# Gated linear attention levels as 64 by 64 products on the two array halves, in one run per head

## The chip, the cores and the metric

The kernel runs on one core of a Trainium2 chip. The metric is the time of one execution on the device, in microseconds (us); a time given for a kernel is the median of several executions. Engines are named as in the profile: PE is the matmul engine and PEld its weight loads, DVE the vector engine, ACT the scalar engine, POOL the general engine, SP the engine that issues most DMAs. Matmuls write to PSUM, eight banks of 128 partitions by 512 float32; DVE and ACT read them there.

## The reference, cut to what matters

One decoder layer on 2048 tokens behind 16 meta tokens, width 1024. A combined projection feeds two branches, a state-space scan (SSD, 16 heads of 64 columns in 4 groups) and gated linear attention (GLA, 4 heads, keys of 128, values of 256). Gates merge the branches, and an output projection and a norm follow. The change is in the GLA branch. Within a chunk it computes

```
gc = cumsum(log_a)                                  # per channel
rel = exp(where(causal, gi[t] - gi[s], -inf))       # per t, s and channel
att = einsum('bhtk,bhsk,bhtsk->bhts', qi, ki, rel)  # scores inside the chunk
o_t = att @ v + (q * exp(g)) @ state
```

The decay between t and s differs by channel, so that `att` isn't one plain product.

## The kernel before, in words

The tokens go in four blocks of 512. For each block (the loop at L1067), a list of "pieces" projects the normed input to what one SSD group or GLA head needs (`proj_conv`, `proj_qk`, `proj_v`, `gla_gates` and so on; their matmuls are L223, L224 and L225 in `accum`, three for each float32 product whose operands are split into high and low parts). Between pieces, `step` (L1012) advances every generator that is running by one `yield`: `ssd_scan` for the four groups, `gla_scan` for the four heads. A scan has more yields than a unit has pieces, so that the last steps of one head fall between the same pieces as the first steps of the next head. After the four blocks come the gates, branch and output products (L1141 to L1349), which the change doesn't touch.

The orders of PE and of SP are written out by hand: they are that of the program (`manual_schedule`, L1066). DVE, ACT and POOL are ordered by a scheduler, which mixes instructions of the scans that are under way. Each engine runs its own order strictly; semaphores make an instruction wait for those of other engines.

A chunk of `gla_scan` has 128 tokens; a block has four chunks, taken as two pairs. The scores are found by levels, at distances 64, 32, 16, 8, 4 and 2. At each level a chunk falls into pairs of neighbouring stretches; the keys of one and the queries of the other are scaled by the decay from the border between them, so that their product gives the scores across this border. `level_in(half)` does the scaling: L858 (DVE) subtracts the border's value, L861 and L862 (ACT) take exponentials, L863 and the two L865 (DVE) multiply by keys and queries into the tile `kq`. For each pair of chunks `kq` is laid out so that one 128 by 128 product serves both: the scores of one chunk stand above the diagonal, and those of the other, transposed, below it. `level_out(half)` makes the two products of a level (L873), a float32 matmul of 128 by 128 by 128 each, into a bank of the pool `pc`. Level 64 is copied to the tile `xa` by ACT (L877); each lower level is merged into `xa` under its mask by a predicated copy on DVE (L880). Levels 64 to 4 come out in the second, third and fourth step of the scan, level 2 in the fifth.

In the fifth step, two products with a matrix of ones (L945) give the scores at distance 1 and 0. L947 merges distance 1 into `xa`; L950 spreads `xa` to the four chunks' `att` under triangular masks; L953 sets the diagonal. L956 splits `att` into high and low parts. In the sixth step, one piece later, PE transposes the two odd chunks of `att` (L960) and goes on to the state update (L965) and the outputs (L981, L982).

Buffers come from pools that rotate: `sq` (six of 128 by 512) holds the temporaries and `kq` of the levels, `att`, and the SSD scan's `dm` and `scm`; `c1` (eight of 128 by 256) holds `xa`, the states and others; `xd` (four) holds the SSD scan's `xdt`. The pool `pc` has two PSUM banks, `pt` three and `pj` three. The SSD scan's product L717 already uses 64 columns at a time: it alternates between the upper and the lower 64 rows of its output.

Of the kernel before, what the change touches and what calls it, by code (L numbers as in the profile page):

```python
# [8 lines left out]
F32 = mybir.dt.float32  # L9
# [17 lines left out]
NSQ = 6  # L27
NT4 = 5
NACT = 8
NC1 = 8  # L30
# [13 lines left out]
def trunk_kernel(ctx: ExitStack, tc: tile.TileContext, xm, xmt, w_feat, w_tok, w_v3, w_zm, w_br, w_o,  # L44
# [7 lines left out]
    def mk(pool, shape, dt, tag, **kw):  # L52
        cnt[0] += 1
        return pool.tile(shape, dt, tag=tag, name=f"{tag}_{cnt[0]}", **kw)
# [575 lines left out]
    def ssd_scan(o, g):  # L630
# [35 lines left out]
        held, intra = {}, {}  # L666

        def before(c):
# [9 lines left out]
            xdt = mk(wk, [P, 4, 64], F32, "xd", bufs=NCH)  # L678
# [7 lines left out]
            dm = mk(wk, [P, 4, P], F32, "sq", bufs=NSQ)  # L686
# [124 lines left out]
    def gla_scan(o, h, last=False):  # L811
# [30 lines left out]
        xa = mk(wk, [P, 2, P], F32, "c1", bufs=NC1)  # L842
        kqs = {}

        def level_in(half):
# [10 lines left out]
            kq = mk(wk, [P, BLK], F32, "sq", bufs=NSQ)  # L856
# [12 lines left out]
        def level_out(half):  # L869
            kq = kqs.pop(half)  # L870
            ps = bank(pc, "pc")
            for r in range(2):
                nc.tensor.matmul(ps[:, r * P:(r + 1) * P], kq[:, 2 * r * P:(2 * r + 1) * P],  # L873
                                 kq[:, (2 * r + 1) * P:(2 * r + 2) * P], start=True, stop=True)
            pv2 = ps[:, :256].rearrange("p (r t) -> p r t", t=P)
            if half == 64:
                nc.scalar.activation(xa, pv2, AF.Copy)  # L877
            else:
                mi = msk[:, LEVELS.index(half)].unsqueeze(1).to_broadcast([P, 2, P])
                nc.vector.copy_predicated(xa, mi, pv2)  # L880
# [20 lines left out]
        level_out(64)  # L901
# [6 lines left out]
        level_out(32)  # L908
        level_in(8)
        level_out(16)  # L910
        level_in(4)
        yield
        level_out(8)
        level_in(2)
        level_out(4)
# [24 lines left out]
        level_out(2)  # L940
        sums_ = []
        for hl, n in parts:
            ps = bank(pt, "pt")
            for i in range(2):
                nc.tensor.matmul(ps[:, :n], ones_r, hl[i], start=i == 0, stop=i == 1)  # L945
            sums_.append(ps)
        nc.vector.copy_predicated(xa, msk[:, len(LEVELS)].unsqueeze(1).to_broadcast([P, 2, P]),  # L947
                                  sums_[0][:, :256].rearrange("p (r t) -> p r t", t=P))
        att = mk(wk, [P, NCH, P], F32, "sq", bufs=NSQ)
        nc.vector.tensor_tensor(att.rearrange("p (r o) t -> p r o t", o=2),  # L950
                                xa.unsqueeze(2).to_broadcast([P, 2, 2, P]),
                                tris.unsqueeze(1).to_broadcast([P, 2, 2, P]), op=ALU.mult)
# [553 lines left out]
def _layout(inputs):  # L1506
# [41 lines left out]
    for i, h in enumerate(LEVELS + (1,)):  # L1548
        if i:
            cmsk[:, i] = (row // (2 * h) == col // (2 * h)) & (row // h != col // h)  # L1550
# [40 lines left out]
```

## Time and profile before

| What | us |
|---|---|
| median of 3 runs (lowest, highest) | 2210.77 (2210.52, 2213.93) |
| the profiled execution, its own time | 2209.51 |
| its span, first to last instruction | 2207.7 |
| PE busy | 2174.5 |
| DVE busy | 1553.8 |
| ACT busy | 1188.5 |
| POOL busy | 693.8 |
| PE busy in the level products L873 (384 records) | 53.4 |
| PE busy in the SSD products L717 (1024 records) | 33.4 |

A float32 matmul that isn't a transpose stands in the profile as two records, since PE passes over it twice. Matmuls are pipelined: a record lasts longer than the step from its start to the next one's start, so that what a matmul costs is read from starts. The span holds 1.8 us less than the execution's own time. The GLA steps of the four blocks lie at about 262 to 436, 610 to 779, 953 to 1122 and 1300 to 1432 us.

### The profile page before, as it was taken

The numbers are of one execution on the slowest core, as the hardware profiler recorded it, in microseconds if no ns is written. First come the engines' busy times: TensorE is split into PE (matmuls) and PEld (weight loads), VectorE is DVE, ScalarE is ACT, GpSimd is POOL, SyncE is SP. The second block draws the span as 40 slices with busy tenths as digits, with TensorE's granted clock in tenths as the row PEclk, the third lists the DMA queues.
The fourth block names the chain that finished last, engine by engine and source line by source line (L and its number), as shares of the span: only waits on it lengthen the run. The fifth ranks groups of instructions, "written<-read, shape, count | busy, mean of one in ns | idle before, by whom it ended". The sixth has DMA issues, their size and how long they took to land.

```text
span 2207.7 us, 35845 instructions
## 1 busy us (share of the span) xinstructions
PE 2174.5 (98%) x12301; PEld 1867.9 (85%) x12301; DVE 1553.8 (70%) x2871; ACT 1188.5 (54%) x2767; POOL 693.8 (31%) x689
## 2 busy tenths in 40 slices
PE   7999999999999999999999999999999999999998
PEld 7999889888888988888988888878888888888887
DVE  5786675677577676658677666674789955789876
ACT  5666655466455456545465554464644545554544
POOL 5444433222222122221222100166233374324341
PEclk9999999999999999999999999999999999999999
DMA  9766775667778677778677664376768866787753
GB/s 316 254 228 235 255 271 211 218 217 244 257 253 265 210 227 230 249 257 274 208 223 238 215 216 161 124 265 214 246 221 297 304 223 216 240 286 255 255 187 121
DMA packets 313702, 518.00 MB, mean 235 GB/s; under 512 B 28080, under 2 KB 162480, under 8 KB 313520
## 3 DMA queue, kind: packets, MB, share of 16 engines
q1 hardware_dynamic: 247008, 419.89, 58.3%
q10 hardware_dynamic: 65872, 93.74, 11.6%
q8 instruction: 96, 1.57, 0.3%
q0 software_dynamic: 640, 2.10, 0.2%
q14 instruction: 86, 0.70, 0.1%
HBM read 368.42 MB, written 147.19 MB: 234 GB/s over the span
## 4 chain that ended last, share of the span: by engine, by line
PE 86%; DVE 4%; ACT 3%; DMA 3%; POOL 1%; issue 1%; SPq 1%; POOLq 0%; ACTq 0%; DVEq 0%
PE pj L223 19%; PE pj L225 19%; PE pj L224 19%; PE pt L225 4%; PE pt L224 4%; PE pt L223 4%; PE pc L223 2%; PE pc L224 2%; PE pc L225 2%; PE pc L873 2%; PE pc L717 1%; PE pc L701 1%; PE pc L981 1%; PE pc L700 1%; DVE acc L612 1%
## 5 line engine op out<-in xcount | busy, mean ns | idle before, releaser
L223 PE MATMUL pj<-ue,whl 128*128 128x512 f32 (+2 forms) x672 | 236.7, 352 | 2.3 <-ACT acc L608 2.2
L224 PE MATMUL pj<-ue,whl 128*128 128x512 f32 (+2 forms) x672 | 228.9, 341 | 0.0
L225 PE MATMUL pj<-ue,whl 128*128 128x512 f32 (+2 forms) x672 | 228.5, 340 | 0.0
L223 PE MATMUL pj<-uo,whl 128*128 128x512 f32 x512 | 206.0, 402 | 0.0
L225 PE MATMUL pj<-uo,whl 128*128 128x512 f32 x512 | 199.9, 390 | 0.0
L224 PE MATMUL pj<-uo,whl 128*128 128x512 f32 x512 | 199.5, 390 | 0.0
L223 PE MATMUL pj<-b,a 128*128 128x512 f32 (+1 forms) x484 | 187.4, 387 | 0.5 <-DVE io L1304 0.5
L224 PE MATMUL pj<-b,a 128*128 128x512 f32 (+1 forms) x484 | 187.4, 387 | 0.0
L225 PE MATMUL pj<-b,a 128*128 128x512 f32 (+1 forms) x484 | 187.4, 387 | 0.0
L612 DVE SCALAR_TENSOR_TENSOR acc<-cin,hcw,acc 128x512 f32<-128x512 f32 (+1 forms) x192 | 156.1, 813 | 29.2 <-ACT acc L608 27.5
L1157 POOL TENSOR_TENSOR as<-ar,ar 128x512 f32<-128x512 f32 x38 | 58.3, 1534 | 371.4 <-DMA ar<-in_w_br 124.7
L83 POOL TENSOR_TENSOR wr<-wr 128x256 f32<-128x256 f32 x80 | 69.7, 871 | 332.2 <-DMA wr<-y 142.0
L1186 DVE TENSOR_TENSOR a<-ar,a 128x512 fp32r<-128x512 f32 x160 | 132.1, 834 | 58.8 <-ACT a L1185 57.8
L223 PEld LDWEIGHTS pj<-ue,whl 128*128 128x128 f32 x672 | 127.2, 189 | 18.3 <-ACT acc L608 3.1
L186 POOL TENSOR_TENSOR whl<-wr,whl 128x512 fp32r<-128x512 f32 (+1 forms) x76 | 102.6, 1357 | 122.0 <-ACT whl L184 93.4
L225 PEld LDWEIGHTS pj<-ue,whl 128*128 128x128 f32 x672 | 127.1, 189 | 14.4
L224 PEld LDWEIGHTS pj<-ue,whl 128*128 128x128 f32 x672 | 127.7, 190 | 13.3
L1186 DVE TENSOR_TENSOR a<-as,a 128x512 fp32r<-128x512 f32 x120 | 104.8, 875 | 41.5 <-ACT a L1185 38.2
L1185 ACT ACTIVATE a<-ar 128x512 fp32r<-128x512 f32 x160 | 99.1, 626 | 58.6 <-PE pt L225 22.1
L1220 ACT ACTIVATE sn<-pj 128x512 f32<-128x512 f32 x118 | 70.2, 595 | 110.8 <-PE pj L225 71.0
L224 PE MATMUL pt<-b,a 128*128 128x512 f32 x320 | 124.5, 389 | 0.0
L225 PE MATMUL pt<-b,a 128*128 128x512 f32 x320 | 124.5, 389 | 0.0
(335 smaller groups left out, 6367.9 us busy)
## 6 DMA issues: line engine op xcount, KB each, us to landing
whl<-k_s SPq DMA_DIRECT2D x96, 512.0 KB, 4.1
whl<-k_g SPq DMA_DIRECT2D x96, 512.0 KB, 4.5
whl<-k_v SPq DMA_DIRECT2D x36, 512.0 KB, 3.8
wr<-in_w_feat SPq DMA_DIRECT2D x64, 256.0 KB, 4.1
k_s<-whl SPq DMA_DIRECT2D x32, 512.0 KB, 3.8
cb<-cumd SPq DMA_DIRECT2D x64, 256.0 KB, 4.7
y<-gg ACTq DMA_DIRECT2D x64, 256.0 KB, 4.2
k_g<-whl SPq DMA_DIRECT2D x32, 512.0 KB, 3.7
```

The source lines that it names most:

```text
L83: nc.gpsimd.tensor_tensor(o, x, y, op=ALU.subtract)
L186: nc.gpsimd.tensor_tensor(hl[:, 1], raw, hl[:, 0].bitcast(F32), op=ALU.subtract)
L223: nc.tensor.matmul(ps, sh, mh, start=first, stop=False, **kw)
L224: nc.tensor.matmul(ps, sh, ml, start=False, stop=False, **kw)
L225: nc.tensor.matmul(ps, sl, mh, start=False, stop=last, **kw)
L612: convd[:] = [nc.vector.scalar_tensor_tensor(acc, cin[:, k:k + tt], hcw[:, ti, k:k + 1], acc, op0=ALU.mult, op1=ALU.add)]
L700: nc.tensor.matmul(ps[:, :256], cf[:, a:a + P], s_ssd[:, g], start=True, stop=True)
L873: nc.tensor.matmul(ps[:, r * P:(r + 1) * P], kq[:, 2 * r * P:(2 * r + 1) * P], kq[:, (2 * r + 1) * P:(2 * r + 2) * P], start=True, stop=True)
L1157: nc.gpsimd.tensor_tensor(s1, a21, a22, op=ALU.add)
L1185: nc.scalar.activation(t[:, 0], src, AF.Copy)
L1186: latest[:] = [nc.vector.tensor_tensor(t[:, 1], src, t[:, 0].bitcast(F32), op=ALU.subtract)]
L1220: nc.scalar.activation(sn, self.ps[n, "a"], AF.Copy)
```

## The change

**The products.** `level_out` goes. `levels_out(att)` makes the products of all six levels in one run, in the fifth step, where level 2 alone was before. Each 128 by 128 product becomes two of 64 columns by 64 columns, since two of its quadrants hold everything that the level's mask lets through: those beside the diagonal for level 64, those on it for the others. The stationary operand is 64 columns wide; the first of the two writes the output's partitions 0 to 63, the second 64 to 127, on the two halves of the array. A head has 24 such products in place of 12. They go to two `pc` banks at once, the first for levels 64 to 8, the second for 4 and 2.

**The merge.** A level now has 64 columns a pair of chunks. Level 64 goes straight to its places in `att` by two ACT copies of 64 partitions, and the opposite places are zeroed by two POOL memsets. ACT copies level 32 to `xa` (64 columns, a pool of its own with one buffer), and DVE merges the other four levels (L892). Distance 1 is merged, and `xa` spread to `att`, in two instructions of 64 partitions each (L957 and L960).

**The buffers.** A pool `kq` with six buffers now holds the `kq` tiles, `dm`, and `xdt` (two chunks to a buffer); `sq` goes from six buffers to three, `c1` from eight to six, and `xd` goes.

```diff
-NSQ = 6
+NSQ = 3
+NKQ = 6
-NC1 = 8
+NC1 = 6
...
-            xdt = mk(wk, [P, 4, 64], F32, "xd", bufs=NCH)
+            if c % 2 == 0:
+                pair[:] = [mk(wk, [P, 2, 4, 64], F32, "kq", bufs=NKQ)]
+            xdt = pair[0][:, c % 2]
...
-            dm = mk(wk, [P, 4, P], F32, "sq", bufs=NSQ)
+            dm = mk(wk, [P, 4, P], F32, "kq", bufs=NKQ)
...
-        xa = mk(wk, [P, 2, P], F32, "c1", bufs=NC1)
+        xa = mk(wk, [P, 2, 64], F32, "xa", bufs=1)
...
-            kq = mk(wk, [P, BLK], F32, "sq", bufs=NSQ)
+            kq = mk(wk, [P, BLK], F32, "kq", bufs=NKQ)
...
-        def level_out(half):
-            kq = kqs.pop(half)
-            ps = bank(pc, "pc")
-            for r in range(2):
-                nc.tensor.matmul(ps[:, r * P:(r + 1) * P], kq[:, 2 * r * P:(2 * r + 1) * P],
-                                 kq[:, (2 * r + 1) * P:(2 * r + 2) * P], start=True, stop=True)
-            pv2 = ps[:, :256].rearrange("p (r t) -> p r t", t=P)
-            if half == 64:
-                nc.scalar.activation(xa, pv2, AF.Copy)
-            else:
-                mi = msk[:, LEVELS.index(half)].unsqueeze(1).to_broadcast([P, 2, P])
-                nc.vector.copy_predicated(xa, mi, pv2)
+        quads = [(slice(i * 64, i * 64 + 64), slice(j * 64, j * 64 + 64)) for i, j in ((0, 0), (1, 1))]
+
+        def levels_out(att):
+            ps = [bank(pc, "pc").rearrange("p (l r t) -> p l r t", r=2, t=64) for _ in range(2)]
+            pl = [ps[n // 4][:, n % 4] for n in range(len(LEVELS))]
+            for n, half in enumerate(LEVELS):
+                kq = kqs.pop(half)
+                for r in range(2):
+                    for i in range(2):
+                        j = 1 - i if half == 64 else i
+                        nc.tensor.matmul(pl[n][i * 64:i * 64 + 64, r],
+                                         kq[:, 2 * r * P + i * 64:2 * r * P + i * 64 + 64],
+                                         kq[:, (2 * r + 1) * P + j * 64:(2 * r + 1) * P + j * 64 + 64],
+                                         start=True, stop=True)
+            for i in range(2):
+                rows, off = slice(i * 64, i * 64 + 64), slice(64 - i * 64, P - i * 64)
+                nc.scalar.activation(att[rows, i::2, off], pl[0][rows], AF.Copy)
+                nc.gpsimd.memset(att[rows, 1 - i::2, off], 0.0)
+            nc.scalar.activation(xa, pl[1], AF.Copy)
+            for n in range(2, len(LEVELS)):
+                nc.vector.copy_predicated(xa, msk[:, n, :64].unsqueeze(1).to_broadcast([P, 2, 64]), pl[n])
...
-        level_out(2)
+        att = mk(wk, [P, NCH, P], F32, "sq", bufs=NSQ)
+        levels_out(att)
...
-        nc.vector.copy_predicated(xa, msk[:, len(LEVELS)].unsqueeze(1).to_broadcast([P, 2, P]),
-                                  sums_[0][:, :256].rearrange("p (r t) -> p r t", t=P))
-        att = mk(wk, [P, NCH, P], F32, "sq", bufs=NSQ)
-        nc.vector.tensor_tensor(att.rearrange("p (r o) t -> p r o t", o=2),
-                                xa.unsqueeze(2).to_broadcast([P, 2, 2, P]),
-                                tris.unsqueeze(1).to_broadcast([P, 2, 2, P]), op=ALU.mult)
+        near = sums_[0][:, :256].rearrange("p (r t) -> p r t", t=P)
+        for rows, on in quads:
+            nc.vector.copy_predicated(xa[rows], msk[rows, len(LEVELS), :64].unsqueeze(1).to_broadcast([64, 2, 64]),
+                                      near[rows, :, on])
+        for rows, on in quads:
+            nc.vector.tensor_tensor(att[rows, :, on].rearrange("p (r o) t -> p r o t", o=2),
+                                    xa[rows].unsqueeze(2).to_broadcast([64, 2, 2, 64]),
+                                    tris[rows, :, on].unsqueeze(1).to_broadcast([64, 2, 2, 64]), op=ALU.mult)
```

The other `level_out` calls and the mask's rows are dropped or cut to match.

**How the instructions move.** In the changed kernel the lines stand lower: L858, L863 and L865 became L861, L866 and L868; L880 became L892, L945 became L953, L947 became L957, L950 became L960, L953 became L963, and PE's transposes L960 became L970. The places shown are in the second block's third head. On PE, the fifth step before, behind the last matmul of a piece (tiles `pj`, `whl`, `uo`):

```order
L225 MATMUL pj_8944<-uo_4617,whl_8959 128x512
L873 MATMUL pc_8982<-sq_8915 128x128 x2
L945 MATMUL pt_8986<-c_1516_8936,ones_r 128x256
L945 MATMUL pt_8986<-c_1517_8937,ones_r 128x256
L945 MATMUL pt_8989<-sq_8940,ones_r 128x512
L945 MATMUL pt_8989<-sq_8941,ones_r 128x512
L223 MATMUL pj_9000<-uo_3929,whl_9001 128x512
```

And now:

```order
L226 MATMUL pj_8986<-uo_4602,whl_9001 128x512
L882 MATMUL pc_9025<-kq_8717 64x64 x4
L882 MATMUL pc_9025<-kq_8790 64x64 x4
L882 MATMUL pc_9025<-kq_8798 64x64 x4
L882 MATMUL pc_9025<-kq_8871 64x64 x4
L882 MATMUL pc_9026<-kq_8879 64x64 x4
L882 MATMUL pc_9026<-kq_8961 64x64 x4
L953 MATMUL pt_9060<-c_1471_8978,ones_r 128x256
```

The ten earlier products of the head, which stood in steps two to four, have come down to here. The transposes that follow stand one piece (24 matmuls of 512 columns) behind in both. On DVE, from the last level's merge to the write of the diagonal, before:

```order
L880 COPY_PREDICATED c_1471_8653<-msk,pc_8982 128x256
L803 SCALAR_TENSOR_TENSOR gg_8973<-gg_8973,pj_8944 128x512
L947 COPY_PREDICATED c_1471_8653<-msk,pt_8986 128x256
L950 TENSOR_TENSOR sq_8993<-c_1471_8653,cst 128x512
L858 TENSOR_TENSOR sq_9159<-g_all_5272 128x512
L953 COPY_PREDICATED sq_8993<-msk,pt_8989 128x512
```

And now, where three merges (L892) with one L861 among them stand just ahead of the first row shown:

```order
L861 TENSOR_TENSOR sq_9335<-g_all_5303 128x512
L892 COPY_PREDICATED xa_8715<-msk,pc_9026 128x128
L866 TENSOR_TENSOR kq_9235<-sq_9234,act_8724 128x4x64
L868 TENSOR_TENSOR kq_9235<-sq_9234,act_8632 128x2x64 x2
L957 COPY_PREDICATED xa_8715<-msk,pt_9060 64x128 x2
L866 TENSOR_TENSOR kq_9336<-sq_9335,act_8724 128x8x32
L868 TENSOR_TENSOR kq_9336<-sq_9335,act_8632 128x2x2x32 x2
L861 TENSOR_TENSOR sq_9343<-g_all_5303 128x512
L960 TENSOR_TENSOR sq_9024<-xa_8715,cst 64x4x64 x2
L861 TENSOR_TENSOR sq_9419<-g_all_5303 128x512
L866 TENSOR_TENSOR kq_9344<-sq_9343,act_8724 128x16x16
L963 COPY_PREDICATED sq_9024<-msk,pt_9063 128x512
```

Before, one instruction of the next head's levels (L858) stood between the merges and L953. Now four L861, three L866 and four L868 of the next head do, and all four merges of lower levels. SP's order is the same in both kernels.

More of the change, by code (lines that the diff above doesn't have):

```diff
@@ L665, in ssd_scan @@
         ssq = mk(sm, [P, 4], F32, "ssq")
-        held, intra = {}, {}
+        held, intra, pair = {}, {}, []
         def before(c):
@@ L900, in gla_scan @@
         level_in(32)
-        level_out(64)
         level_in(16)
@@ L907, in gla_scan @@
             nc.vector.tensor_copy(s_gla[:, h], ps[:, :256])
-        level_out(32)
         level_in(8)
-        level_out(16)
         level_in(4)
         yield
-        level_out(8)
         level_in(2)
-        level_out(4)
         def halves(t):
@@ L1549, in _layout @@
         if i:
-            cmsk[:, i] = (row // (2 * h) == col // (2 * h)) & (row // h != col // h)
+            near = (row % 64 // (2 * h) == col // (2 * h)) & (row % 64 // h != col // h)
+            cmsk[:, i] = near & (col < 64)
     def pcol(v):
```

## The prediction

> **What bounds the kernel now.** I read the page first: which engine is full, and whose work the chain that ended last is made of.
>
> ```profile
> span 2207.7 us, 35845 instructions
> PE 2174.5 (98%) x12301; PEld 1867.9 (85%) x12301; DVE 1553.8 (70%) x2871; ACT 1188.5 (54%) x2767; POOL 693.8 (31%) x689
> PE 86%; DVE 4%; ACT 3%; DMA 3%; POOL 1%; issue 1%; SPq 1%; POOLq 0%; ACTq 0%; DVEq 0%
> ```
>
> PE is busy for 98% of the span and makes up 86% of the chain. A microsecond taken from PE is a microsecond of the time, as long as PE then finds its next operands ready. The view of PE's waits, whose two longest rows follow, shows how seldom it does not:
>
> ```profile
> PE pt L333 <- DMA cst<-in_cf: 10.3, 1, 10.3
> PE pj L223 <- ACT acc L608: 4.3, 4, 2.1
> ```
>
> One wait is the start of the kernel; nothing later comes to 5 us in total. No wait stands in that view before the transposes of `att` (L960), the place where this change will be felt. So two things count: what PE saves, and whether `att` still comes before PE wants it.
>
> **What PE saves.** The level products and their nearest relative, the SSD products that already run on the two halves, in the view of groups by line:
>
> ```profile
> L873 PE MATMUL pc<-sq 128*128 128x128 f32 x384 | 53.4, 276 | 0.0
> L717 PE MATMUL pc<-xd,sq 128*64 128x64 f32 x1024 | 33.4, 224 | 0.0
> ```
>
> The busy times hold the pipelined tails, so I take the cost from starts. The timeline of PE around four level products (eight records):
>
> ```profile
> 713.93 0.28 PE L225 MATMUL pj<-whl,uo 128*128 128x256 f32 x1
> 714.04 1.05 PE L873 MATMUL pc<-sq 128*128 128x128 f32 x8
> 714.85 0.36 PE L223 MATMUL pj<-whl,uo 128*128 128x256 f32 x1
> 715.05 0.28 PE L224 MATMUL pj<-whl,uo 128*128 128x256 f32 x1
> ```
>
> From L225's start to L224's is 1.12 us. Two steps of the projection take 0.23 of it (0.11 to 0.12 each), which leaves 0.89 for eight passes, 0.111 each. A head has 24: 2.67 us. Now a run on halves:
>
> ```profile
> 1293.17 0.39 PE L225 MATMUL pj<-uo,whl 128*128 128x512 f32 x1
> 1293.49 2.08 PE L717 MATMUL pc<-xd,sq 128*64 128x64 f32 x64
> 1295.51 0.50 PE L223 MATMUL pj<-uo,whl 128*128 128x512 f32 x1
> 1295.84 0.39 PE L224 MATMUL pj<-uo,whl 128*128 128x512 f32 x1
> ```
>
> Here it is 2.67 us, less two steps of 0.227: 2.21 for 64 passes. The first and the last of them start 1.86 apart (2.08 less the 0.22 of one record), 0.0296 a pass; the other 0.32 us is what entering and leaving the mode costs. The new products have L717's shape and its alternation of halves. A head makes 48 passes in one run: 1.42 + 0.32 = 1.74 us. The saving is 0.93 a head, **15 us** over 16 heads. By busy time it would be more (53.4 against 768/1024 of 33.4, 28 us); that counts tails which the next matmul covers, and I keep it only as an outer bound.
>
> **What the merge costs.** The transposes are due one piece after the last level. In the same head as the order shown above, PE:
>
> ```profile
> 727.83 0.60 PE L873 MATMUL pc<-sq 128*128 128x128 f32 x4
> 728.19 0.48 PE L945 MATMUL pt<-c,ones_r 128*128 128x256 f32 x2
> ...
> 734.43 0.39 PE L960 MATMUL pt<-cst,sq 128*128 128x128 f32 x2
> ```
>
> and DVE:
>
> ```profile
> 728.47 0.45 DVE L880 COPY_PREDICATED c<-msk,pc 128x256 f32<-128x256 uint8 x1 [4.34 <-PE pc L873]
> 728.82 0.68 DVE L803 SCALAR_TENSOR_TENSOR gg<-gg,pj 128x512 f32<-128x512 f32 x1
> 729.41 0.44 DVE L947 COPY_PREDICATED c<-msk,pt 128x256 f32<-128x256 uint8 x1
> 729.88 0.69 DVE L950 TENSOR_TENSOR sq<-c,cst 128x512 f32<-128x512 f32 x1
> 730.49 0.68 DVE L858 TENSOR_TENSOR sq<-g_all 128x512 f32<-128x512 f32 x1
> 731.09 0.73 DVE L953 COPY_PREDICATED sq<-msk,pt 128x512 f32<-128x512 uint8 x1
> 731.71 0.41 DVE L863 TENSOR_TENSOR sq<-sq,act 128x256 f32<-128x256 f32 x1
> 732.04 0.68 DVE L858 TENSOR_TENSOR sq<-g_all 128x512 f32<-128x512 f32 x1
> 732.64 0.49 DVE L865 TENSOR_TENSOR sq<-sq,act 128x128 f32<-128x128 f32 x2
> 733.05 0.42 DVE L273 TENSOR_TENSOR atp<-sq,atp 128x256 fp32r<-128x256 f32 x1
> ```
>
> `att` is done at 731.82, and PE comes for it at 734.43: 2.6 us to spare, with one L858 of the next head in between. After the change PE comes 1.74 + 6.24 (728.19 to 734.43), about 7.9 us behind the run's start. `att` takes this:
>
> - *To the first merge, 1.85 us.* ACT waits for the first bank's 16 products, 32 passes of 0.0296 and a tail of 0.22 (1.2 us), then makes three copies of 128 columns, of which the last is `xa`. Copies of that size (first row below) take 0.27, so that in a row they add 0.65.
> - *The chain's own rows, 3.0 us.* A predicated copy takes 0.45 for 256 columns and 0.73 for 512, so 0.30 for 128: four merges at 0.27 from start to start (1.1), distance 1 in two (0.45), the spreading in two of 256 columns (0.41 like L863, 0.7 together), L963 (0.73).
> - *The next head's rows that now stand between, 4.2 us.* Four L861 at 0.60, three L866 at 0.33, four L868 at 0.205, by the starts above.
>
> Together 9.05 us: `att` is 1.15 us late. That is the cheap end, since these DVE rows were undisturbed. The groups of DVE in the second block's GLA part (610 to 779 us) give the dear end, and prices of rows that stand between in other heads:
>
> ```profile
> L685 ACT ACTIVATE bt<-pt 128x128 f32<-128x128 f32 x64 | 17.4, 271 | 18.1 <-DVE tok L682 18.1
> L858 DVE TENSOR_TENSOR sq<-g_all 128x512 f32<-128x512 f32 x22 | 16.1, 732 | 0.1
> L865 DVE TENSOR_TENSOR sq<-sq,act 128x128 f32<-128x128 f32 x46 | 12.2, 306 | 0.0
> L863 DVE TENSOR_TENSOR sq<-sq,act 128x256 f32<-128x256 f32 x23 | 11.6, 505 | 6.9 <-ACT sq L861 4.5 <-PE pc L873 2.4
> L351 DVE SCALAR_TENSOR_TENSOR acc<-acc,pv,cin 128x512 f32<-128x512 f32 x8 | 6.4, 802 | 5.8 <-DMA acc<-in_xmt 5.8
> L356 DVE TENSOR_TENSOR ue<-acc,ue 128x512 fp32r<-128x512 f32 x8 | 5.9, 732 | 1.5 <-ACT ue L354 1.4
> L803 DVE SCALAR_TENSOR_TENSOR gg<-gg,pj 128x512 f32<-128x512 f32 x7 | 4.8, 681 | 5.7 <-ACT gg L802 5.7
> ```
>
> With 0.73, 0.51 and 0.31 in place of 0.68, 0.41 and 0.28, the eleven rows take 0.55 more and the wait is 1.7. I take 1.4. PE waits in order, so the piece behind the transposes is late by as much; DVE does the same work either way, so the next head gains nothing back.
>
> I read the changed order of DVE between the same two places for every head and priced the rows alike. Five heads have this one's rows: 7.0 us. The first heads of blocks two and three have one L866 fewer, and PE has eight SSD transposes more to do before: 0.4 together. The second heads of these blocks have an L352 (0.8) more: 2.1 each, 4.2. The very first head has an L352, an L357, an L806 and two L868 more: 4.0. The fourth heads of blocks one to three have no next head in the queue, and wait for nothing. In the last block the heads crowd together: in its second head, DVE reaches the first merge 2.6 us later and has some twenty rows up to L963, 5.8; the third head 1.0; the fourth, with a short piece before the transposes, 1.4. **Sum of the waits: 24 us**, between 19 and 31 by the two sets of prices.
>
> The rest I cost at nothing. The memsets are 32 on a POOL that is 31% busy, due only four microseconds later; the nearest small POOL row is this:
>
> ```profile
> L610 POOL COPY tails<-cin 128x3 f32<-128x3 f32 x64 | 14.1, 221 | 162.4 <-ACT cin L607 162.2
> ```
>
> At 0.22, or 0.8 behind one 256-column POOL row, they hide behind the merge; late, they would add up to 0.8 a head, 13 us. ACT loses one copy and gains three a head, on an engine at 54%. Both `pc` banks are taken at once, but the merges that free them end ahead of `att`, before PE wants one again. Fewer buffers in `sq` and `c1` can only hold DVE and ACT back on instructions that the sum has in its order already; `dm` and `xdt` fit the six `kq` buffers that one SSD group fills, and are read before the next group comes. I give these together 0, and 3 us either way for the range.
>
> **Sum.** The profiled execution took 2209.51, its span and 1.8 around it. 2209.5 - 15 + 24 = 2218.5. The median of the three runs shown is 1.3 above that execution, so the forecast is **2220 us**.
>
> A rule of the Trainium skill bears on the two longest waits. The row first, PE's granted clock in 40 slices:
>
> ```profile
> PEclk9999999999999999999999999999999999999999
> ```
>
> It stands at nine tenths or more throughout, and PE had no wait over 3 us after the start. TensorE: Matmul & The Clock Gate, in its part on the HAM clock gate, says that an idle window of about 3.4 us halves PE's clock until PE has been busy for as long. By it the two waits of 4.0 and 5.8 us would each cost up to 1.7 us more, an estimate from that page, and the sum would be 2223; no run here shows it.
>
> **The rivals.**
>
> *The merge keeps up* (other side). The eleven rows of the next head might fill DVE time that would be idle anyway (it sat idle 4.34 us before L880 in the rows above), and `att` would lie inside PE's 7.9 us. It decides at that point: the rows between first merge and L963 would have to take 6.0 us in place of 7.2. For it: 2.6 us to spare before. Against: DVE is in order, and those rows stand behind merges that can't start until PE's run is half done. Then 2210.8 - 15, **2196 us**. Chance 0.15.
>
> *A draw.* Merges of 128 columns and half the partitions come nearer to 0.22 than to 0.30, and rows run at their shortest: 0.5 us less a head in twelve heads, waits of 18 us, about as much as PE saves. **2213 us**. Chance 0.21.
>
> *POOL and ACT are late too.* DVE rows at their dear end, memsets or ACT copies behind other work, 31 + 8 us: **2235 us**. For it, L863 waits on ACT's L861 in the rows above. Chance 0.13.
>
> *The halves don't overlap* (the change doesn't do what it says). The two products of a pair read different operands, while L717 streams the same one to both halves. If each pass took 0.111, a head would cost 5.3 + 0.3 in place of 2.67: +47 us, less the waits that a later PE then no longer has: **2255 us**. Against it, every pass of L717 loads weights of its own as these do. Chance 0.02.
>
> **How the numbers follow.** The forecast, waits that come to more than PE saves, has 0.49 (2215 to 2228). A measurement of this kernel can tell 0.2%, 4.4 us, from no change. Faster by more than that is the first rival, 0.15. Within it is most of the draw and a little of the forecast, 0.22; slower the rest, 0.63. The range runs from 2204, short of the first rival, to 2234, for the dear end; it leaves out 0.2.
>
> **What would show it.** In the profile of the changed kernel: L882 with 768 records at 25 us of busy time, and runs of 48 from whose start to L953's start is about 1.5 us (else the first term is wrong). A row in PE's waits that was not there, L970 behind DVE L963 (or the split's ACT row), in 11 to 13 heads, 1 to 2 us in most and 4 to 6 in two: if this row is missing, the forecast's second term falls and the time is near 2196. POOL L889 or ACT L888 as the releaser would mean the third rival. New waits at L700, L701 or L676 would mean that the smaller pools, costed at nothing, are what counts.

## The result and the profile after

The changed kernel takes **2266.59 us** (median of 4 runs, 2265.25 to 2268.03), beside 2210.64 for the kernel before on the same chip (4 runs). The ratio is 1.0253, with a 95% interval of 1.0235 to 1.0271: 56 us slower. The forecast was 2220, its range 2204 to 2234; the sign was right and the size was not.

The page of the changed kernel, the lines that answer to those shown of before:

```profile
span 2263.4 us, 36718 instructions
PE 2173.0 (96%) x12685; PEld 1854.3 (82%) x12685; DVE 1542.3 (68%) x2887; ACT 1195.9 (53%) x2799; POOL 702.1 (31%) x721
PE 66%; DVE 8%; DMA 7%; ACT 3%; issue 2%; POOL 1%; SPq 0%; ACTq 0%; POOLq 0%; DVEq 0%
```

PE's busy time is hardly less, although the level products fell from 53.4 us of it to 26.1. Its idle time rose from 33 to 90 us (span less busy time), and PE's share of the chain fell from 86% to 66%. The view of PE's waits says where, in us in total, times and the longest:

```profile
PE pt L970 <- DVE sq L963: 51.7, 15, 12.5
PE pj L224 <- ACT acc L609: 4.9, 3, 2.9
PE pc L703 <- DVE s_ssd L707: 3.3, 3, 1.1
PE pt L499 <- ACT sq L490: 3.1, 3, 1.1
PE pt L970 <- ACT act L833: 1.8, 1, 1.8
```

The first row is the wait that the prediction named, at twice the size. L703 and L499 are new too: before, neither stood in that view. PE's timeline in the head that the prediction worked through:

```profile
753.21 1.62 PE L882 MATMUL pc<-kq 128*64 128x64 f32 x48
754.76 0.50 PE L953 MATMUL pt<-c,ones_r 128*128 128x256 f32 x2
755.10 0.63 PE L953 MATMUL pt<-sq,ones_r 128*128 128x512 f32 x2
763.01 0.41 PE L970 MATMUL pt<-cst,sq 128*128 128x128 f32 x2 [1.83 <-DVE sq L963]
```

The 48 passes take 1.55 us to the next product's start, as forecast. PE came for `att` 7.97 us behind the run's start (763.01 - 1.83 - 753.21; forecast 7.9) and waited 1.83 (forecast 1.15 to 1.7). So this head came out nearly as worked out. The head ahead of it did not. DVE there:

```profile
705.25 0.75 DVE L352 SCALAR_TENSOR_TENSOR acc<-acc,pv,cin 128x512 f32<-128x512 f32 x1 [1.55 <-DMA acc<-in_xmt]
706.70 0.69 DVE L357 TENSOR_TENSOR ue<-acc,ue 128x512 fp32r<-128x512 f32 x1 [0.70 <-ACT ue L355]
707.31 0.68 DVE L806 SCALAR_TENSOR_TENSOR gg<-gg,pj 128x512 f32<-128x512 f32 x1
707.93 0.64 DVE L892 COPY_PREDICATED xa<-msk,pc 128x128 f32<-128x128 uint8 x2
...
713.16 1.21 DVE L861 TENSOR_TENSOR sq<-g_all 128x512 f32<-128x512 f32 x1
714.29 1.39 DVE L960 TENSOR_TENSOR sq<-xa,cst 64x256 f32<-64x256 f32 x2
715.71 0.69 DVE L861 TENSOR_TENSOR sq<-g_all 128x512 f32<-128x512 f32 x1
...
717.43 0.72 DVE L963 COPY_PREDICATED sq<-msk,pt 128x512 f32<-128x512 uint8 x1
```

Its run starts at 704.29. The first merge comes 3.64 us later (2.09 in the other head), and rows of 0.68 and 0.86 us take 1.21 and 1.39. POOL works at that time:

```profile
712.10 1.72 POOL L84 TENSOR_TENSOR wr<-wr,wr 128x256 f32<-128x256 f32 x2
713.90 1.05 POOL L84 TENSOR_TENSOR wr<-wr 128x256 f32<-128x256 f32 x1
```

`att` is 14 us behind the run, and PE waits 6.04. Groups of heads, waits in us, each from the row of its L970:

| Heads | forecast | measured |
|---|---|---|
| the very first | 4.0 | 12.5 |
| five with the rows of the head worked through | 7.0 | 10.3 |
| first heads of blocks two and three | 0.4 | 8.6 |
| second heads of blocks two and three | 4.2 | 12.1 |
| fourth heads of blocks one to three | 0 | 1.3 |
| the other three of the last block | 8.2 | 8.7 |

### The profile page after: what moved, and what is told of

It is laid out like the page before. It is cut to its first block, busy times and chain, and to the rows that moved or that the text cites. A ratio compares the mean times of both kernels' runs of the same rounds, so it can differ in the third digit from the quotient of the medians.

```text
span 2263.4 us, 36718 instructions
## 1 busy us (share of the span) xinstructions
PE 2173.0 (96%) x12685; PEld 1854.3 (82%) x12685; DVE 1542.3 (68%) x2887; ACT 1195.9 (53%) x2799; POOL 702.1 (31%) x721
## 4 chain that ended last, share of the span: by engine, by line
PE 66%; DVE 8%; DMA 7%; ACT 3%; issue 2%; POOL 1%; SPq 0%; ACTq 0%; POOLq 0%; DVEq 0%
PE pj L224 14%; PE pj L226 14%; PE pj L225 14%; PE pt L226 4%; PE pt L225 4%; PE pt L224 4%; PE pc L224 2%; PE pc L225 2%; PE pc L226 2%; DMA y<-gg 1%; DVE sq L861 1%; DMA br<-out_t 1%; PE pc L991 1%; DMA io<-g 1%; PE pc L720 1%
## 5 line engine op out<-in xcount | busy, mean ns | idle before, releaser
L225 PEld LDWEIGHTS pj<-ue,whl 128*128 128x128 f32 x672 | 127.7, 190 | 13.5
L1195 ACT ACTIVATE a<-ar 128x512 fp32r<-128x512 f32 x160 | 98.5, 624 | 53.3 <-PE pj L226 20.7
L224 PE MATMUL pt<-b,a 128*128 128x512 f32 x320 | 124.3, 389 | 0.0
L226 PE MATMUL pt<-b,a 128*128 128x512 f32 x320 | 124.3, 389 | 0.0
L225 PE MATMUL pt<-b,a 128*128 128x512 f32 x320 | 124.3, 389 | 0.0
```

The costliest lines, as they stand in the source:

```text
L224: nc.tensor.matmul(ps, sh, mh, start=first, stop=False, **kw)
L225: nc.tensor.matmul(ps, sh, ml, start=False, stop=False, **kw)
L226: nc.tensor.matmul(ps, sl, mh, start=False, stop=last, **kw)
L1195: nc.scalar.activation(t[:, 0], src, AF.Copy)
```

## The experiments

The theory at this point: DVE's order, with the next head's level rows ahead of the diagonal, makes the waits, and a late first merge and stretched rows enlarge them. The rivals: the merge chain alone is late; the array halves cost clock by themselves; the smaller pools cost something after all. Each ratio below is to the kernel before on the same chip, where it took 2207.9 to 2209.7 us, so that runs are best compared by their ratios. The granted clock is the share of its full clock that PE had, by the profile; it was 0.997 over the kernel before and 0.987 over the changed one.

**Rows behind the diagonal.**

```diff
+            with tc.issue_after(diag[-1].ins) if diag else nullcontext():   # the subtraction of level_in
+        diag[:] = [nc.vector.copy_predicated(att, msk[:, 0]...)]
```

> The changed kernel, with one constraint for DVE's scheduler: the subtractions L862 of a head's levels may only come behind the previous head's write of the diagonal. Nothing else is changed; no row of the next head's levels then stands between the merges and that write, but for three in the last block's second head. Theory (the order of DVE makes the waits): the eleven rows, 4.2 us at their shortest and more where POOL works beside them, leave the stretch; what is left is the late first merge of five heads (up to 2.2 us more) and the chain's own 3.0 us, which fit into PE's 7.9. The waits before the transposes fall from 53 us to under 10, most of it in the first head, the half-clock stretches behind them go too, and the time is 2210.6 - 15 + 5 to 10, about 2200 to 2206. Rival one (the merge chain itself is late, by ACT's copies and by stretched DVE rows): a head whose first merge comes 4.3 us behind the run's start still waits 1 to 3 us, and the time is 2225 to 2235. Rival two (runs on the array halves lower the granted clock by themselves): the waits go, the clock stays at 0.987, and the time is near 2220.

2222.82 us, ratio 1.0063 (1.0045 to 1.0080). Of 56 us, some 42 are gone. PE's waits at the transposes (L971 here), and DVE in the head worked through:

```profile
PE pt L971 <- DVE sq L964: 9.1, 8, 3.6
```

```profile
734.53 1.38 DVE L893 COPY_PREDICATED xa<-msk,pc 128x128 f32<-128x128 uint8 x4 [0.56 <-ACT xa L891]
736.02 0.63 DVE L958 COPY_PREDICATED xa<-msk,pt 64x128 f32<-64x128 uint8 x2
736.67 0.87 DVE L961 TENSOR_TENSOR sq<-xa,cst 64x256 f32<-64x256 f32 x2
737.68 0.74 DVE L964 COPY_PREDICATED sq<-msk,pt 128x512 f32<-128x512 uint8 x1
```

The bare chain is done 5.99 us behind the run (at 732.43), 3.67 earlier than with the eleven rows (4.2 forecast for them). The waits fell as the theory said, and the granted clock rose to 0.995, which speaks against the second rival although the time lies near its 2220. But the time stayed 17 us above the 2206 at the theory's upper end. PE's idle time is still 23 us more than in the kernel before, and only 9 of it stands before the transposes; the next run bears on the rest.

**The buffers alone**, in the kernel before.

```diff
-NSQ = 6
+NSQ = 3
+NKQ = 6
-NC1 = 8
+NC1 = 6
+            (xdt, dm and kq from the pool kq, as in the change)
```

> The kernel before with the buffers of the changed one alone: sq with three buffers, c1 with six, and a pool of six for the kq tiles, dm and xdt. The level products and their merges stay as they were. The prediction costed this at nothing: 2210.6, within 3. Rival (the smaller pools hold DVE and ACT back): new waits of PE at the SSD products or at the level products, and a time of 2215 or more.

2226.64 us, ratio 1.0076 (1.0051 to 1.0102), some 17 us, by the interval 11 to 22: the rival holds. With the level products and their merges as before, PE's waits have these rows; in the kernel before, the wait for `c` (there L969) came to 2.8, and the other two did not stand:

```profile
PE pc L224 <- DVE c L972: 6.8, 5, 2.0
PE pt L499 <- ACT sq L490: 3.5, 3, 1.6
PE pc L703 <- DVE s_ssd L707: 3.3, 3, 1.1
```

What became late at L499 is seen on ACT: before, the row that fills `sq` for the gates stood ahead of the scaling of `ot`, and now behind it. Before, then with the smaller pools:

```profile
460.83 0.57 ACT L489 ACTIVATE sq<-pt 16x512 fp32r<-16x512 f32 x1
461.31 0.62 ACT L691 ACTIVATE sq<-sq 128x512 f32<-128x512 f32 x1
461.83 0.39 ACT L689 ACTIVATE sq<-cb,tkc 128x128 f32<-128x128 f32 x1
462.12 1.30 ACT L993 ACTIVATE ot<-ot,rstd 128x256 f32<-128x256 f32 x3
```

```profile
464.27 1.31 ACT L996 ACTIVATE ot<-ot,rstd 128x256 f32<-128x256 f32 x3 [0.41 <-POOL rstd L269]
465.49 0.49 ACT L996 ACTIVATE ot<-ot,rstd 128x256 f32<-128x256 f32 x1
465.88 0.57 ACT L490 ACTIVATE sq<-pt 16x512 fp32r<-16x512 f32 x1
```

There, fewer buffers did not hold an instruction back in an order that stayed; the scheduler made another order. What made the other two waits was not followed up.

**`c1` alone.** `NC1 = 6` in the kernel before, nothing else.

> The kernel before with c1 cut from eight buffers to six and nothing else. All three cuts of buffers together cost 17 us, with PE waiting 4 us more for states in c1 (L972), and 7 us at L499 and L703 where it had not waited. If the c1 cut costs only the waits that name it, 2212 to 2215; if it carries nearly all of the 17, 2222 or more, and the waits at L499 and L703 appear too; if the sq cut carries all, 2208.

2208.88 us, ratio 0.9994 (0.9981 to 1.0006). The 17 us are not `c1`'s; they belong to the regrouping of `sq`, `kq` and `xd`, or to that together with `c1`; no run separates these.

**Transposes one piece later**, ahead of the outputs, in the changed kernel.

> The changed kernel with the transposes of att one piece later, ahead of the outputs; the first state update, which does not need att, changes places with them. DVE's order is kept, so the next head's rows still stand between the merges and the diagonal. A piece lasts some 5 to 6 us. Theory (att is late by DVE's order, and lateness is all that it costs): waits of up to 6.1 us go, the first head keeps some 6 of its 12.5, and the odd chunks' split, now directly ahead of its use, may cost up to 0.5 us a head: 2210.6 - 15 + 6 + (0 to 8), about 2202 to 2210. Rival (the halves lower the clock by themselves): clock 0.987 still and a time near 2220. If DVE were the bound over the whole head, the waits would only move to the outputs, and the time would stay above 2250.

2260.18 us, ratio 1.0231 (1.0214 to 1.0249). This is a miss of both: `att`'s own wait fell to 7.4 us, but another stands in its place.

```profile
PE pc L226 <- DVE atp L274: 19.4, 17, 2.8
PE pc L224 <- ACT atp L273: 10.0, 11, 2.5
```

The split of the odd chunks, transposes to ACT to DVE to PE, was hidden by a piece. Directly ahead of its use it costs nearly 2 us a head, not the 0.5 at most that I allowed. The third case named there, DVE as the bound over the whole head, would also give a time above 2250; against it stands the run with the rows behind, where the same DVE rows leave waits of 9 us before the transposes. This run by itself doesn't decide between the two.

**The halves at the old places**, one level a step, with the buffers of before.

> The halves alone: the products are the 64 by 64 ones of the change and the merge is its compact one, but every level comes out in the step where it stood before, and sq, c1 and xd are those before. Level 64 is kept in a c1 tile until att exists. PE then enters the half mode in four runs a head (64; 32 and 16; 8 and 4; 2) in place of one. If each entry costs the 0.32 us of the prediction, a head takes 48 x 0.0296 + 4 x 0.32 = 2.70 us against 2.67 before, so nothing is gained: 2208 to 2213, with 0 to 5 us of waits from the rows that now stand ahead of the diagonal. Rival (the gain is in the smaller products, and the entry is not paid per run): up to 1.25 us a head less, about 2188 to 2193.

2220.82 us, ratio 1.0050 (1.0035 to 1.0065), above the theory's 2208 to 2213. The rival is out: the waits at the transposes (6.8 and 3.9 us, more than expected) are as much as the 11 us lost, so that the smaller products saved about nothing when the mode was entered four times a head.

**Two runs a head, buffers of before, rows behind the diagonal.** Levels 64, 32 and 16 in the third step, 8, 4 and 2 in the fifth.

> A kernel put together from the parts: 64 by 64 products in two runs a head (levels 64, 32 and 16 in the third step, 8, 4 and 2 in the fifth), so that at most three kq tiles are held and the buffers of before are enough (sq six, c1 eight, xd four); and the next head's level rows on DVE stay behind the diagonal. By the theory PE takes 1.42 + 2 x 0.32 = 2.06 us a head in place of 2.67, 10 us less; the late merge has three levels and fits into PE's piece; what is left of waits before the transposes is 0 to 6: 2198 to 2204. Rival one (six sq buffers do not suffice for three held tiles): waits at L499, L703 or at the level products, 2210 to 2220. Rival two (keeping the rows behind costs DVE what it lacks later): waits for states or atp of more than 6 us, about 2208.

2210.80 us, ratio 1.0004 (0.9991 to 1.0017): a draw, and neither theory's number. It is 12 us under the kernel of one run with the small pools; if the second entry costs 16 x 0.32 = 5, the buffers are again worth some 17, by subtraction between two kernels that differ in both. PE's busy time is 10 us less than in the kernel before, as the theory had it, but its idle time is 9.5 more: single waits at the transposes (3.1), for `atp` (2.2) and for a state (L676, 4.4 where it was 2.4) are the largest that grew.

**The same without the constraint.**

> The kernel with two runs a head and the buffers of before (2210.8 us), but with DVE's order left to the scheduler again: two to five of the next head's rows and more stand between the last merges and the diagonal. Theory (rows ahead of the diagonal make att late, whatever the buffers are): waits before the transposes of 1 to 3 us in ten heads come back, 15 to 25 us in all, and 2222 to 2235. Rival (with three levels in the late run and larger pools there is slack enough): 2206 to 2212.

2246.63 us, ratio 1.0171 (1.0155 to 1.0187). The waits are back, more than expected: with the right buffers and a late merge of only three levels, DVE's order alone costs 36 us.

```profile
PE pt L972 <- DVE sq L965: 37.3, 13, 8.8
```

**The same with the constraint later**, behind the second split in place of the diagonal.

> The kernel with two runs a head, the buffers of before and the next head's level rows behind, now behind the second split of att (L274's row one piece later) in place of behind the diagonal, so that they are not ahead of that split and of the states. In the former, PE still waited 1 to 1.6 us for atp and for states in the first two heads of blocks two and three. If that is where its saving of 10 us went, 2204 to 2208; if the run-to-run scatter and single waits elsewhere are all there is, 2209 to 2213 again; if DVE then lacks the time for levels 64 to 16, new waits at the first run, and 2215 or more.

2213.38 us, ratio 1.0016 (1.0006 to 1.0027). No gain: the waits for `atp` went, but those at the transposes rose to 13.5 us.

**POOL's rows left out**, in the changed kernel.

> The changed kernel without the 32 by 2 rows of POOL (make_sums, L84) that run while the GLA heads of blocks two and three are under way: these subtractions for later stages are left out, their transfers are not. DVE's order between merges and diagonal stays as in the changed kernel. In those two blocks the first and second heads waited 4.2 to 6.1 us, and DVE's rows there took 1.21 us in place of 0.68 while L84 ran, in the third heads 0.68 and 1.83 us of waiting. Theory (POOL's rows stretch DVE's beside them): the four waits lose 2 to 3 us each, the half-clock stretches behind them are halved, and the time falls by 10 to 14, to 2253 to 2257. Rival (these rows are slow, and att late, for another reason: transfers, or ACT's queue alone): 2264 to 2268, and L862-like rows of 1.2 us stay.

2260.08 us, ratio 1.0227 (1.0208 to 1.0246), some 6 us less where 10 to 14 were expected. The rows are what was said: in the second block's second head every level row of 128x512 takes 0.68 to 0.69 us, and the stretch from first merge to `att` fell from 10.2 to 8.2 us. The four waits fell only from 20.7 to 17.8, since the first merges came later still (3.9 to 5.1 us, where they had come at 3.6 to 4.3). From first merge to `att`, the four heads lost 5 us together.

**First copy on DVE**, in the kernel with the rows behind.

> The kernel with the next head's rows behind the diagonal (2222.8 us), and in it the first copy to xa on DVE in place of ACT. In that kernel the first merge still came 4.0 to 5.0 us behind the run's start in four heads, where ACT stood in other work, and 2.10 in the others; 7.7 of its 9.1 us of waits before the transposes are in heads with a late first merge. Theory (ACT's order makes the first merge late): the first merge comes at about 1.7 in every head but the first and the last, those waits go, and the time falls by 3 to 5, to 2218 to 2220. Rival (DVE itself is late there): no change, 2221 to 2224.

2222.24 us, ratio 1.0057 (1.0036 to 1.0078): no change. The first merge came at 3.7 to 4.5 us in the same four heads, and at 4.8 in one more. The theory fell: not ACT's copy, but DVE too stands behind something. In the changed kernel ACT, in a head whose run starts at 655.11:

```profile
657.57 0.60 ACT L805 ACTIVATE gg<-pj 128x512 f32<-128x512 f32 x1 [5.05 <-DMA y<-gg]
658.07 0.59 ACT L769 ACTIVATE act<-pj 128x512 f32<-128x512 f32 x1
658.54 0.55 ACT L888 ACTIVATE sq<-pc 64x128 f32<-64x128 f32 x2
659.12 0.28 ACT L890 ACTIVATE xa<-pc 128x128 f32<-128x128 f32 x1
```

L805 waits for a store out of a `gg` buffer, and the copies, and DVE's L806, stand behind L805.

**Stores that leave `gg` free.**

> The changed kernel with the stores of both branches' y reading a constant in place of the gg buffer (the y that later stages read is then not the computed one). As many bytes go out, but a gg buffer is free when its last engine has read it, not when its store has landed. Theory (the first merge comes late because ACT's L805 waits for the store of a gg buffer, and L888, L890 and DVE's L806 stand behind it): the first merge comes at 2.1 to 2.6 us in the first and second heads of blocks two and three, where it came at 3.6 to 4.3; their waits of 4.2 to 6.1 fall by 1.5 to 2.2 each, the first head's 12.5 by more, and the time to 2250 to 2258. Rival (L805 is held by something else, the store only ends last by the profile): first merges at 3.6 to 4.3 still, 2264 to 2268.

2317.06 us, ratio 1.0485 (1.0469 to 1.0502). The time says nothing: stores that wait for no result were put at the kernel's start, where ACT's rows for the first weights waited for them, and PE was 55 us late by 100 us. From there on the traces can be compared. In the first heads the first merge came at 2.1 us, where it had come at 4.3, and their waits fell from 4.4 and 4.2 to 2.6 and 2.5: there, the store is the cause. In the second heads it came at 2.8 and 3.0, where it had come at 3.6 and 4.2, and the waits fell only from 6.0 and 6.1 to 5.5 and 5.7. Something else holds these. In the changed kernel, in the head whose run starts at 704.29, ACT's L805 and the copies stand behind this row:

```profile
706.04 0.63 ACT L355 ACTIVATE ue<-acc 128x512 fp32r<-128x512 f32 x1 [3.06 <-DVE acc L352]
```

DVE's L352, shown above, had itself waited 1.55 us for a load of `in_xmt`; in the third block's second head it waited 3.43. No run takes this wait away.

**Filling the waits.** Three runs of the changed kernel with idle products ahead of the transposes.

```diff
+        for _ in range({(0, 0): 160, (1, 0): 48, (1, 1): 72, (2, 0): 48, (2, 1): 72, (3, 1): 72}.get((o.b, h), 0)):
+            nc.tensor.matmul(ps[:, :P], ones_r, ones_r, start=True, stop=True)
```

> The changed kernel with idle work for PE just ahead of the transposes, in the six heads whose wait there was over 4 us: 48 to 160 products of 128 columns of ones, into the bank that the transposes then overwrite. They take most of each wait, without PE being late for att. Theory (a wait over 3 to 4 us also costs what PE then loses at half clock): steps of 512 columns behind these waits took 0.427 in place of 0.213 us, three to nine of them a wait, some 8 us in all; the half-clock stretches go, the granted clock rises from 0.987 towards 0.997, and the time falls by 7 to 10, to about 2257 to 2260. Rival (the half clock only marks the idle time and costs nothing of its own): 2266, within 3.

> Idle work for PE ahead of the transposes again, with fewer products: 80, 20 and 36 in place of 160, 48 and 72. In the run before, each took 0.11 us and not the 0.06 assumed, so the filling was longer than the waits. It now takes 8.9, 2.2 and 4.0 us of waits of 12.5, 4.2 to 4.4, and 6.0, and att is not held up. Theory (what PE loses at half clock behind a long wait is a cost of its own): the half-clock stretches behind these six waits go and 6 to 9 us with them, 2257 to 2261. Rival (no cost of its own): 2266, within 3.

> Idle work for PE ahead of the transposes once more, as long as the wait itself: 108, 37, 52, 35, 52 and 52 products at 0.111 us for the waits of 12.5, 4.4, 6.0, 4.2, 6.1 and 6.1 us. With half of it, each wait still left 1.8 to 3.4 us of idle time and half-clock stretches of 3.4 us came all the same. Theory (the half clock behind the waits costs what the slow steps show, 6 to 7 us in all): the stretches go, and 2259 to 2262. Rival (no cost of its own): 2266, within 3.

2282.91, 2267.51 and 2272.93 us; ratios 1.0342 (1.0316 to 1.0368), 1.0261 (1.0246 to 1.0276) and 1.0283 (1.0258 to 1.0307). None came where a theory put it. The second lies in its rival's band, but it doesn't test the rival, since the half-clock stretches stayed. The first filling was longer than the waits (52 us for 32 saved), the second left 1.3 to 3.4 us of five of the six, and half-clock stretches came all the same. In the third, the stretches behind the waits of blocks two and three went. From the second transpose to the 31st product behind it PE took 6.27 us in each of these four heads, where it had taken 8.56, 7.57, 8.81 and 7.66. So the slow steps have a price of 1.3 to 2.5 us where they stand. Part of it was lost again further on: from the first head's run to the third's, PE gained 1.0 us in block two and 1.7 in block three. In the last block the filling itself ran at half clock, 52 products in 10.65 us:

```profile
1426.24 10.65 PE L970 MATMUL pt<-ones_r 128*128 128x128 f32 x52 [1.93 <-DVE xa L957]
```

What the half clock costs of the whole time is not settled by these runs.

**A fifth `gg` buffer**, paid for with the `c1` cut that costs nothing, in the kernel of two runs.

> The kernel with two runs a head, the buffers of before and the next head's rows behind the diagonal (2210.8), with c1 at six buffers, which cost nothing by itself, and the space given to a fifth gg buffer. If the stores of gg are what still holds ACT and DVE in it (its first head waits 2.6 us, single waits of 1 to 1.6 elsewhere), 2203 to 2207, under the kernel before by more than 0.1%. If not, 2208 to 2213, the same as both.

2206.72 us, ratio 0.9989 (0.9977 to 1.0001). The first head's wait went from 2.6 to 0.9 us. This is the fastest version, 2 us under the kernel before, but its interval touches 1: not told from no change.

## Why the prediction was wrong, by its own steps

**What bounds the kernel: right.** PE's lateness became the time nearly one to one: its idle time grew by 57 us, the span by 56.

**What PE saves, 15 us: right**, by the run of 1.55 us quoted above, and by the halves at the old places, where four entries a head ate the whole saving.

**The waits, 24 us: the step that failed most.** They came to 53.5 (51.7 and 1.8). The mechanism was right: put the rows behind the diagonal and these waits fall to 9.1, the time by some 42; leave the order to the scheduler in the kernel of two runs and 36 come back. The sizes were about right wherever the rows ran undisturbed (1.83 us for 1.4, the last block 8.7 for 8.2). They failed in the very first head and in the first and second heads of blocks two and three, which waited 24.6 us more than forecast, mainly on two terms:

- *"To the first merge, 1.85 us"*, taken for every head but the second of the last block. It was 2.1 in the undisturbed heads and 3.6 to 8.4 in these five, 15.6 us late in all. In the first heads ACT waits for a store out of a `gg` buffer, in the second for DVE, which waits for a load. The trace of before had a warning. Its ACT, in the first heads of blocks one to four:

```profile
289.86 0.60 ACT L802 ACTIVATE gg<-pj 128x512 f32<-128x512 f32 x1 [3.14 <-DMA y<-gg]
...
641.52 0.60 ACT L802 ACTIVATE gg<-pj 128x512 f32<-128x512 f32 x1 [3.14 <-DMA y<-gg]
...
983.90 0.60 ACT L802 ACTIVATE gg<-pj 128x512 f32<-128x512 f32 x1 [2.88 <-DMA y<-gg]
...
1323.02 0.60 ACT L802 ACTIVATE gg<-pj 128x512 f32<-128x512 f32 x1 [3.45 <-DMA y<-gg]
```

  These waits cost PE nothing before. In blocks two and three L802 ended 0.2 and 0.4 us ahead of the head's level product (642.28 and 984.86), in block four over 3 us ahead. I moved two more copies and all lower levels' merges behind this place and read ACT's durations, not its waits. The wait itself was also longer in the changed kernel: 5.05 and 5.28 us in blocks two and three, and it lasted until 2.4 to 2.5 us behind the run's start; in block four it still cost nothing. So the trace of before showed which wait to fear, not its size. The third rival had "ACT copies behind other work", at 0.8 us for POOL and ACT together.
- *The prices of DVE's rows.* I took the mean of a whole block as the dear end (0.73 for 0.68). Where POOL works beside them, rows take up to 1.21 and not a few per cent more. POOL's rows come in groups of four, 20 to 30 us apart in blocks two and three. In the changed kernel a group falls between the run and the diagonal in the first and second heads, none in the third, and only the end of that stretch meets one in the fourth. A mean hides that, but single rows of the trace of before had shown it, as this one beside a group of POOL's from 647.0 to 650.7:

```profile
648.89 1.21 DVE L858 TENSOR_TENSOR sq<-g_all 128x512 f32<-128x512 f32 x1
```

  Leaving POOL's rows out gave some 6 us of time, and 5 us in these stretches. With the 15.6 above, 4 us of the 24.6 stay open. (By its own prices the dear end adds 0.62 us and not the 0.55 written there; that changes little.)

**"The rest I cost at nothing": wrong for the buffers, by 17 us in the kernel before.** The sentence that fewer buffers "can only hold DVE and ACT back on instructions that the sum has in its order already" was the fault. The order was read between merges and diagonal only; the smaller pools changed it elsewhere, as at L499. The sign that the prediction named is there: L703, before's L700, is a new wait. In the changed kernel not all of the 17 us show: outside the transposes, PE's idle time is only 4 us more than before. The wait for `c` (6.8 us in the run with the buffers alone) has no row there; that a PE already late no longer meets it is likely, not shown.

**Half clock, left out of the sum.** Behind the waits of 4 us and more PE's steps were slow. The timeline behind the 6.04 us wait, which ended at 718.30, from 720.46 on:

```profile
720.46 0.63 PE L225 MATMUL pj<-uo,whl 128*128 128x512 f32 x1
720.89 0.60 PE L226 MATMUL pj<-uo,whl 128*128 128x512 f32 x1
721.32 0.40 PE L224 MATMUL pj<-uo,whl 128*128 128x512 f32 x1
721.56 0.40 PE L225 MATMUL pj<-uo,whl 128*128 128x512 f32 x1
```

The steps are 0.43 us and then 0.23. In the stretches of granted clock 0.5 around the six waits over 4 us PE was busy for 24.8 us, so that some 12 us are lost there. That is worked out from the trace of the changed kernel; the third filling bears it out behind four of the waits, and for the whole time no experiment does. The prediction's view in 40 slices could not show such stretches: a slice is 55 us, and one stretch of 3.4 us at half clock leaves it at 0.97, a 9. The kernel before has three of them, at 107.3, 233.6 and 305.3 us, behind waits of 2.1, 2.4 and 2.1 us.

The sum as measured: -15 for the products; +57 for PE's idle time, of which 53.5 stand before the transposes and 4 elsewhere; and +12 for the half clock, 35 us of busy time at it in place of 10. That is 54, against 56 between the spans. The terms were forecast as -15, 24 and 0.

## What to carry to other kernels

When work moves behind a place in an engine's order, read which instruction at that place waits in the trace of before, however free that wait is there: it can become a price of all that is put behind it, and a larger one. Price rows at the place and time where they will run, not by a mean, and cost a cut of buffers as a new order of every engine that the scheduler sets. A run on the array halves pays once per entry, so gather products only as far as buffers and the merge behind them allow; here two runs with the old buffers and the next head's rows held back came out even, and one run with small ones, its rows left to the scheduler, lost 56 us.

## What the runs showed of the hardware

- A DVE row of 128x512 with both inputs in SBUF took 0.68 to 0.69 us, and up to 1.21 while a POOL row with two inputs in SBUF ran beside it; without the POOL rows it took 0.69 at the same place. The Trainium skill, GPSIMD Engine Reference, Specifications, says that POOL and DVE share SBUF interfaces and contend where a DVE instruction has two SBUF inputs; the trace agrees and gives the price, which I had not looked for.
- A wait shorter than I had taken for harmless can be followed by half clock. In the kernel with the rows behind, behind a wait of 2.35 us that ended at 705.18, the columns being length, PE's busy time, granted clock, DMA share and GB/s:

```profile
699.80:703.20 3.40, 3.02 (x16) 1.00 0.81 275
703.20:706.60 3.40, 1.42 (x9) 1.00 0.43 169
706.60:710.00 3.40, 3.40 (x10) 0.50 0.20 77
710.00:713.40 3.40, 3.40 (x17) 1.00 0.54 146
```

  The clock fell after the wait, for one stretch of 3.4 us, with PE busy throughout. The Trainium skill, TensorE: Matmul & The Clock Gate, Part 1, has windows of this length that run freely and halve the clock after an idle one. The length agrees; here the window was 1.42 us busy and not idle, and still the clock fell. The length of a wait doesn't settle it: behind one of 2.94 us in the changed kernel (it ended at 357.7) the clock stayed at 1.00.
- Entering the half mode fits what the prediction read from the SSD products, 0.32 us each time: with one entry a head 48 passes took 1.55 us to the next product's start, and with four entries nothing of the saving was left.
